# A hybrid encoder block: the rounded weight chunks at places of their own in the line, and the fetch of h's sums on GpSimd's queue

## The chip, the cores and the metric

The kernel runs on one core of a Trainium2 chip. The metric is the device time of one execution in microseconds. Beside the times there is one profiled execution, from which all rows of the profile come. The engines go by their names in the profile: PE is TensorE's matrix multiplier (PEld its weight load), DVE is VectorE, ACT is ScalarE, POOL is GpSimd, SP is SyncE, which only issues DMAs here. A "q" behind a name (SPq) means the engine's sequencer, which waits and issues.

## What is computed

One layer of a streaming encoder, in float32, for 256 tokens of width 2048. Attention heads and a convolution work side by side on one input projection, and a gated feed-forward part follows:

```
xn   = rms_norm(x) @ w_in                          # 2048 x 5120: q, k, v and the two halves ga, gg
att  = diff_attention(rope(q), rope(k), v)         # 4 heads, block-causal
u    = silu(layer_norm(conv31(ga * sigmoid(gg))))  # 1024 channels, 31 causal taps
h    = x + concat(att, u) @ w_out                  # 2048 x 2048
hn   = rms_norm(h)
y    = h + (silu(hn @ w_gate) * (hn @ w_up)) @ w_down   # 2048 x 5632, 2048 x 5632, 5632 x 2048
```

## The kernel before

All weights are read once, as float32. TensorE multiplies in a rounded float32 form, so each weight chunk `w` is split in two: `whi`, the chunk rounded, and `wlo = w - whi`, its residue; the activations are split in the same way (`xhi`/`xlo`, `ahi`/`alo` and so on). A product is made of three matmuls: hi by hi, lo by hi and hi by lo, the activations stationary and 512 columns of the weights streaming.

The work is a list of 337 **chunks** in a fixed order, and `run_chunks` walks through it. For each chunk `t` it emits the loads, roundings and splits of chunks some steps ahead, then the matmuls of `t`. A *plain* chunk has 128 x 1024 weights (two k-tiles of 512 columns):

- `load_chunk` loads it with one DMA from SyncE's queue into a buffer of the tag `raw` (RAW_BUFS of them). Chunks marked `spare_raw`, every third one in many stretches, take one of the two larger `wb` buffers in its place. In `w_gate`, `w_up` and the last twelve chunks of `w_out` none is marked.
- `round_chunk` copies it to `whi` on ScalarE. For some chunks (`by_dma`) ScalarE also writes the negative to `wlo`, and a DMA from GpSimd's queue adds the raw weights to it from memory, which gives the residue.
- `split_chunk` makes the residue `wlo` on VectorE for the others.
- `multiply` or `multiply_two` runs the matmuls; the first two products read `whi`, the last reads `wlo`.

`whi` and `wlo` have four buffers each (HL_BUFS), taken in turn. A raw buffer is free again once its chunk is split. SyncE works through its DMAs in order and stands still wherever the buffer of the next one is not free.

The layer's feed-forward part works in three groups of 4, 4 and 3 blocks of 512 hidden columns (FGROUPS). Block 0 uses plain chunks; the ten others are *fast blocks*, which use a scheme with seven products for half of the contraction: 4 pair chunks (`s`, 1 MB each, always in `wb`) and 8 plain ones each. After a group come the plain chunks of its `w_down` rows: four output blocks of 512 columns (`n` = 0 to 3), eight chunks each, in the last group six. The activations that these need are the last step of a block: `block_done` makes the gated product in the buffers `sum0` to `sum3`, and `transposed` has TensorE transpose them in two halves (L827), ScalarE round each half (`ahi`, L829) and VectorE make its residue (`alo`, L831). So that the engines stay busy these steps are spread over the chunks that follow (TO_TRANSPOSE and `lag`); the last chunk of the output block of a group is the first that needs the second half.

The running sum of h lies in the output in memory: groups 0 and 1 add their parts to it by accumulating DMAs from GpSimd (L1034). In the last group, `fetch_sums` reads it back into buffers of the tags `sum0` to `sum3` (two for each output block), VectorE adds the product to it in `down_done` (L1043), and a DMA writes the finished columns (L1044, on GpSimd's queue but for the last block). The first fetch stands in the order of work at the fifth chunk of the group's first output block, behind the loads that run two chunks ahead; the later ones each stand at the first chunk of their block:

```
            if g == len(FGROUPS) - 1:
                fetch_at[at + (0 if n else FGROUPS[g] * N // P // NK - 2)] = n
```

All tiles of some size have lengths that are multiples of 512 bytes (LINE is 128 floats), so they lie at the same place of a 512-byte line.

Of the kernel before, what the change touches and what calls it, by code (L numbers as in the profile page):

```python
# [12 lines left out]
F32 = mybir.dt.float32  # L13
F32R = mybir.dt.float32r
# [4 lines left out]
P = 128  # L19
# [12 lines left out]
N = 512  # L32

LINE = 128
# [14 lines left out]
NK = 2  # L49
# [5 lines left out]
CONV_BLOCKS = (1, 1, 2, 2, 2)  # L55

AHEAD = 2
RAW_BUFS = 5
AUX = 4

LAG = (3, 2, 6)
HL_BUFS = 4

KTILE_US = 1.30
TAP_US = 0.396
# [35 lines left out]
def tile_block(  # L101
# [6 lines left out]
    act, dve, pool, pe, sp = nc.scalar, nc.vector, nc.gpsimd, nc.tensor, nc.sync  # L108

    const = ctx.enter_context(tc.tile_pool(name="const", bufs=1))  # L110
    small = ctx.enter_context(tc.tile_pool(name="small", bufs=4))

    lhs = ctx.enter_context(tc.tile_pool(name="lhs", bufs=KD // 2))
    wp = ctx.enter_context(tc.tile_pool(name="wp", bufs=4))
# [141 lines left out]
    def spend(us):  # L256
        credit[0] -= us
# [19 lines left out]
    def block(w, cols, ks, xs, done=None, bkey=None, first=True, last=True, spare=False, cuts=()):  # L277

        ks = list(ks)
        cols = [(cols, N)] if isinstance(cols, int) else cols  # L280
        width = sum(n for _, n in cols)
        bkey = bkey if bkey is not None else ("b", len(chunks))
        i = 0
        cuts = list(cuts)
        while i < len(ks):
            part = ks[i : i + (cuts.pop(0) if cuts else NK * N // width)]
            i += len(part)
            chunks.append(dict(w=w, k0=part[0], nk=len(part), cols=cols, width=width, xs=xs, bkey=bkey,
                               first=part[0] == ks[0] and first, last=last and i == len(ks),
                               done=done if i == len(ks) else None, spare=spare, by_dma=False,  # L290
                               load=load_chunk, round=round_chunk,
                               split=split_chunk, multiply=multiply))
# [11 lines left out]
    def load_chunk(c):  # L304
# [4 lines left out]
        else:  # L309
            c["raw"] = view(wp.tile([P, NK * N], F32, tag="raw", name="raw", bufs=RAW_BUFS))  # L310
        ks = c["ks"] if "ks" in c else range(c["k0"], c["k0"] + c["nk"])
        c["src"] = src = weights([(c["w"], k, col, n) for k in ks for col, n in c["cols"]])
        sp.dma_start(out=c["raw"].rearrange("p k n -> p (k n)"), in_=src)

    def round_chunk(c):
        c["hi"] = c["view"](wp.tile([P, NK * N], F32R, tag="whi", name="whi", bufs=HL_BUFS))
        act.copy(c["hi"], c["raw"])  # L317
        if c["by_dma"]:
            c["lo"] = c["view"](wp.tile([P, NK * N], F32R, tag="wlo", name="wlo", bufs=HL_BUFS))
            act.activation(c["lo"], c["raw"], AF.Copy, scale=-1.0)  # L320
            pool.dma_start(out=c["lo"].rearrange("p k n -> p (k n)"), in_=c["src"].bitcast(F32R), accum_op=ALU.add)

    def split_chunk(c):
        if not c["by_dma"]:
            c["lo"] = c["view"](wp.tile([P, NK * N], F32R, tag="wlo", name="wlo", bufs=HL_BUFS))
            dve.tensor_tensor(c["lo"], c["raw"], c["hi"].bitcast(F32), ALU.subtract)  # L326
            spend(LO_US * c["nk"] * c["width"] / N)

# [55 lines left out]
    def run_chunks():  # L384
# [16 lines left out]
        for t in range(n):  # L401
            load_lead, dma_lead, hi_lead, lo_lead = lead(t)
            while split < min(rounded[0], t + 1 + lo_lead):
                chunks[split]["split"](chunks[split])
                split += 1
            while loaded < min(n, t + 1 + load_lead):
                load(loaded)
                loaded += 1
                if load_lead == lo_lead:
                    do_round(1, loaded)  # L410
                    do_round(0, loaded)
                    chunks[split]["split"](chunks[split])
                    split += 1
            do_round(1, t + 1 + dma_lead)
            do_round(0, t + 1 + hi_lead)
            while split < min(n, t + 1 + lo_lead):
                chunks[split]["split"](chunks[split])
                split += 1
            if t in fetch_at:
                fetch_sums(fetch_at[t])  # L420
            chunks[t]["multiply"](chunks[t])
            if chunks[t].get("prompt") and chunks[t]["done"]:
                resume()
# [537 lines left out]
    def fast_block(j, order, after_down):  # L961

        units, sums = [], {}
        left = dict(s=list(range(NS)), g=list(TWOS), u=list(TWOS))
        for unit in order:
            kind = unit.lower()
            what = left[kind].pop(0)
            c = dict(kind=kind, sums=sums, done=None, first={}, last={})
            if kind == "s":
                c.update(k=what, col=j * N, by_dma=False, load=load_pair, round=round_pair, split=split_pair,  # L970
                         multiply=multiply_pair, uses=[q for q, _, _ in PRODUCTS], products=PRODUCTS)
            else:
                c.update(ks=what, w="w_gate" if kind == "g" else "w_up", nk=2, width=N, cols=[(j * N, N)],
                         by_dma=unit.isupper(),
                         load=load_chunk, round=round_chunk, split=split_chunk, multiply=multiply_two,
                         uses=(Q3, QX) if kind == "u" else (Q2, Q4))
            units.append(c)
        assert not any(left.values())
        if after_down:

            units[0]["products"] = PRODUCTS[4:] + PRODUCTS[:4]
        for q in range(8):
            users = [c for c in units if q in c["uses"]]
            users[0]["first"][q] = users[-1]["last"][q] = True
        [c for c in units if c["kind"] == "s"][-1]["done"] = products_done
        units[-1].update(done=lambda sums: block_done(j, sums), prompt=True)
        chunks.extend(units)
# [33 lines left out]
    def fetch_sums(n):  # L1021
        so_far[n] = []
        for m in range(NM):
            t = ffn["pool"].tile([P, N], F32, tag=f"sum{n % 2 * NM + m}", name="so_far")
            sp.dma_start(out=t, in_=out[m * P : (m + 1) * P, n * N : (n + 1) * N])
            so_far[n].append(t)

    def down_done(g, n, ps):
# [99 lines left out]
```

## Time and profile before

| | |
|---|---|
| median of 3 runs | 1083.91 us (1081.84 to 1084.14) |
| the profiled execution | 1078.51 us, span 1076.7 us |
| granted TensorE clock, mean | 0.995 |
| raw loads (L313) | 295 of 512 KB, median 4.9 us to landing |
| pair loads (L898) | 40 of 1024 KB, median 6.2 us to landing |
| residues by DMA (L321) | 48 of 512 KB, median 8.3 us to landing |
| fetches of h's sums (L1025) | 8 of 256 KB, median 4.4 us to landing |

The span runs from the first to the last instruction; the profiled execution's own time is a little longer. Rows of the timeline begin with the start and the length in microseconds, then engine, line, operation, output and inputs by the program's names; brackets hold how long the engine was idle before, and what ended that. Rows of the waits give the total, the number and the longest wait.

### The profile page before, as it was taken

The numbers are of one execution on the slowest core, as the hardware profiler recorded it, in microseconds if no ns is written. First come the engines' busy times: TensorE is split into PE (matmuls) and PEld (weight loads), VectorE is DVE, ScalarE is ACT, GpSimd is POOL, SyncE is SP. The second block draws the span as 40 slices with busy tenths as digits, with TensorE's granted clock in tenths as the row PEclk, the third lists the DMA queues.
The fourth block names the chain that finished last, engine by engine and source line by source line (L and its number), as shares of the span: only waits on it lengthen the run. The fifth ranks groups of instructions, "written<-read, shape, count | busy, mean of one in ns | idle before, by whom it ended". The sixth has DMA issues, their size and how long they took to land. (4 is left out here: it accounts for less than half of the span.)

```text
span 1076.7 us, 13151 instructions
## 1 busy us (share of the span) xinstructions
PE 1051.7 (98%) x4834; PEld 870.9 (81%) x4834; DVE 801.4 (74%) x979; ACT 618.0 (57%) x811; POOL 110.4 (10%) x155
## 2 busy tenths in 40 slices
PE   8999999999999999999999999999999999999798
PEld 7988888877888887788888878878888878888686
DVE  4799988899666689988644688889745477897353
ACT  6544566756756557757343667586544474765231
POOL 0130112200100100101000111010001010100000
PEclk9999999999999999999999999999999999999899
DMA  9555555344457568898476898988847799887471
GB/s 314 205 176 180 200 189 176 137 176 151 143 190 242 175 228 252 284 304 244 153 232 197 267 295 252 293 221 268 259 157 201 239 277 319 223 273 208 145 278 66
DMA packets 62781, 236.57 MB, mean 220 GB/s; under 512 B 7044, under 2 KB 8510, under 8 KB 57596
## 3 DMA queue, kind: packets, MB, share of 16 engines
q1 hardware_dynamic: 52320, 202.66, 52.1%
q0 software_dynamic: 10336, 33.04, 16.6%
q8 instruction: 38, 0.62, 0.2%
q14 instruction: 27, 0.22, 0.1%
q10 hardware_dynamic: 60, 0.03, 0.0%
HBM read 227.30 MB, written 8.39 MB: 219 GB/s over the span
## 5 line engine op out<-in xcount | busy, mean ns | idle before, releaser
L317 ACT CAST whi<-raw 128x1024 fp32r<-128x1024 f32 (+1 forms) x297 | 305.8, 1050 | 183.2 <-PE acc L357 98.1
L326 DVE TENSOR_TENSOR wlo<-raw,whi 128x1024 fp32r<-128x1024 f32 (+1 forms) x249 | 299.7, 1219 | 142.8 <-ACT whi L317 140.9
L357 PE MATMUL acc<-whi,alo 128*128 128x512 f32 x384 | 150.5, 392 | 6.6 <-DVE alo L831 6.6
L356 PE MATMUL acc<-whi,ahi 128*128 128x512 f32 x384 | 150.4, 392 | 0.0
L356 PE MATMUL acc<-whi,xhi 128*128 128x512 f32 (+1 forms) x352 | 131.0, 378 | 3.2 <-ACT xhi L223 2.4
L357 PE MATMUL acc<-whi,xlo 128*128 128x512 f32 (+1 forms) x352 | 129.5, 374 | 0.5 <-DVE xlo L224 0.4
L949 PE MATMUL q<-whi,chi 128*128 128x512 f32 x320 | 124.7, 390 | 0.0
L950 PE MATMUL q<-whi,clo 128*128 128x512 f32 x320 | 124.6, 389 | 0.0
L932 PE MATMUL q<-wh,fhi 128*128 128x512 f32 x280 | 109.7, 392 | 1.7 <-DVE alo L831 1.7
L934 PE MATMUL q<-wl,fhi 128*128 128x512 f32 x280 | 109.0, 389 | 0.0
L933 PE MATMUL q<-wh,flo 128*128 128x512 f32 x280 | 109.0, 389 | 0.0
L512 DVE SCALAR_TENSOR_TENSOR y<-upad,cw,y 128x256 f32<-128x256 f32 x240 | 103.7, 483 | 4.4 <-ACT y L505 3.9
L362 PE MATMUL acc<-wlo,ahi 128*128 128x512 f32 x384 | 103.6, 391 | 0.0
L911 ACT CAST wh<-wt 128x2048 fp32r<-128x2048 f32 x40 | 76.5, 1912 | 38.3 <-DVE wt L909 37.6
L916 DVE TENSOR_TENSOR wl<-wt,wh 128x2048 fp32r<-128x2048 f32 x40 | 91.7, 2291 | 6.6 <-ACT wh L911 5.9
L915 DVE TENSOR_TENSOR wl<-wb,wh 128x1536 fp32r<-128x1536 f32 x40 | 70.1, 1754 | 27.9 <-ACT wh L910 27.9
L357 PEld LDWEIGHTS acc<-whi,alo 128*128 128x128 f32 x384 | 72.6, 189 | 22.1 <-DVE alo L831 6.9
L362 PE MATMUL acc<-wlo,xhi 128*128 128x512 f32 (+1 forms) x352 | 88.3, 376 | 1.4 <-DVE wlo L326 1.4
L955 PE MATMUL q<-wlo,chi 128*128 128x512 f32 x320 | 86.6, 392 | 2.8 <-DMA wlo<-in_wts_dram 2.8
L356 PEld LDWEIGHTS acc<-whi,ahi 128*128 128x128 f32 x384 | 72.5, 189 | 15.3 <-ACT ahi L829 0.2
L362 PEld LDWEIGHTS acc<-wlo,ahi 128*128 128x128 f32 x384 | 71.7, 188 | 14.6
L356 PEld LDWEIGHTS acc<-whi,xhi 128*128 128x128 f32 x352 | 67.2, 191 | 14.9 <-ACT xhi L223 2.8
(197 smaller groups left out, 1487.2 us busy)
## 6 DMA issues: line engine op xcount, KB each, us to landing
raw<-in_wts_dram SPq DMA_DIRECT2D x295, 512.0 KB, 4.9
wb<-in_wts_dram SPq DMA_DIRECT2D x40, 1024.0 KB, 6.2
wlo<-in_wts_dram POOLq DMA_DIRECT2D x48, 512.0 KB, 8.3
out_dram<-part POOLq DMA_DIRECT2D x16, 256.0 KB, 5.1
out_dram<-h POOLq DMA_DIRECT2D x8, 256.0 KB, 5.9
so_far<-out_dram SPq DMA_DIRECT2D x8, 256.0 KB, 4.4
h<-in_x_dram SPq DMA_DIRECT2D x6, 256.0 KB, 7.6
out_dram<-so_far POOLq DMA_DIRECT2D x6, 256.0 KB, 3.0
```

Source lines behind the costliest of these rows:

```text
L317: act.copy(c["hi"], c["raw"])
L326: dve.tensor_tensor(c["lo"], c["raw"], c["hi"].bitcast(F32), ALU.subtract)
L356: pe.matmul(ps[m], xhi[:, ms], hi[:, j, :], start=c["first"] and j == 0, stop=False)
L357: pe.matmul(ps[m], xlo[:, ms], hi[:, j, :], start=False, stop=False)
L362: pe.matmul(ps[m], xhi[:, ms], lo[:, j, :], start=False, stop=c["last"] and j == nk - 1)
L512: dve.scalar_tensor_tensor(y[:, ct, :], src, wk, y[:, ct, :], ALU.mult, ALU.add)
L916: dve.tensor_tensor(c["lo"][:, :4], c["t"], c["hi"][:, :4].bitcast(F32), ALU.subtract)
L932: pe.matmul(ps, fhi[:, f, p, :], c["hi"][:, w], start=bool(first), stop=False)
L933: pe.matmul(ps, flo[:, f, p, :], c["hi"][:, w], start=False, stop=False)
L934: pe.matmul(ps, fhi[:, f, p, :], c["lo"][:, w], start=False, stop=bool(last))
L949: pe.matmul(ps, x1[:, ms], hi[:, i, :], start=i == 0 and bool(c["first"].get(q)), stop=False)
L950: pe.matmul(ps, x2[:, ms], hi[:, i, :], start=False, stop=False)
```

## The change

The four `whi` and the four `wlo` buffers are now separate tags of one buffer each. Each but one is a line (512 bytes) longer and is used from an offset of its own on: 16, 32, 288 and 352 bytes for `whi`, 0, 256, 384 and 448 bytes for `wlo`. They are taken in the same turn as before. An unused tile of 384 bytes in the first pool moves everything behind it, so that the pools of weights start at a line. RAW_BUFS goes from five to four, which gives the room. The fetch of h's sums in the last group (L1025) is issued by GpSimd's queue in place of SyncE's.

```
-RAW_BUFS = 5
+RAW_BUFS = 4
...
+SHIFTS = dict(whi=(4, 8, 72, 88), wlo=(0, 64, 96, 112))
...
     const = ctx.enter_context(tc.tile_pool(name="const", bufs=1))
+    const.tile([P, 3 * LINE // 4], F32, tag="to_line", name="to_line")
...
+    turns = dict(whi=0, wlo=0)
+
+    def shifted(tag):
+        i = turns[tag] % HL_BUFS
+        turns[tag] += 1
+        o = SHIFTS[tag][i]
+        return wp.tile([P, NK * N + (LINE if o else 0)], F32R, tag=f"{tag}{i}", name=tag, bufs=1)[:, o : o + NK * N]
+
     def round_chunk(c):
-        c["hi"] = c["view"](wp.tile([P, NK * N], F32R, tag="whi", name="whi", bufs=HL_BUFS))
+        c["hi"] = c["view"](shifted("whi"))
         act.copy(c["hi"], c["raw"])
         if c["by_dma"]:
-            c["lo"] = c["view"](wp.tile([P, NK * N], F32R, tag="wlo", name="wlo", bufs=HL_BUFS))
+            c["lo"] = c["view"](shifted("wlo"))
...
     def split_chunk(c):
         if not c["by_dma"]:
-            c["lo"] = c["view"](wp.tile([P, NK * N], F32R, tag="wlo", name="wlo", bufs=HL_BUFS))
+            c["lo"] = c["view"](shifted("wlo"))
...
             t = ffn["pool"].tile([P, N], F32, tag=f"sum{n % 2 * NM + m}", name="so_far")
-            sp.dma_start(out=t, in_=out[m * P : (m + 1) * P, n * N : (n + 1) * N])
+            pool.dma_start(out=t, in_=out[m * P : (m + 1) * P, n * N : (n + 1) * N])
```

## The prediction

> **What bounds the kernel now.** I read the page's head first, then TensorE's waits and the longest holes between matmuls, then the chain that ended last around the longest hole, then SyncE's waits.
>
> ```profile
> span 1076.7 us, 13151 instructions
> ...
> PE 1051.7 (98%) x4834; PEld 870.9 (81%) x4834; DVE 801.4 (74%) x979; ACT 618.0 (57%) x811; POOL 110.4 (10%) x155
> ```
>
> TensorE is busy 98% of the span, so time is won or lost in two ways only: in the 25 us where it has nothing to do, or in what one matmul takes. The windows show where a good part of those 25 us lies (columns: stretch, its length, busy us and count of PE, PEld, DVE, ACT, POOL, granted clock, DMA share, GB/s):
>
> ```profile
> 1011.00:1015.00 4.00, 1.60 (x9) 1.03 (x7) 0.00 (x0) 0.59 (x1) 0.00 (x0) 1.00 0.58 183
> 1015.00:1019.00 4.00, 0.00 (x0) 0.00 (x0) 1.64 (x2) 2.09 (x2) 0.00 (x0) 0.56 0.97 327
> 1019.00:1023.00 4.00, 3.76 (x10) 3.03 (x11) 0.19 (x1) 0.44 (x1) 0.00 (x0) 0.59 1.01 410
> ...
> 1027.00:1072.00 45.00, 45.00 (x200) 37.28 (x199) 19.43 (x20) 13.72 (x13) 2.16 (x4) 1.00 0.46 164
> ```
>
> An undisturbed matmul takes 45.00/200 = 0.225 us. From 1012 to 1019 us there is none, and the granted clock falls to 0.56 and stays low (0.59) behind the hole. The timeline has the edges, the chain has the reason:
>
> ```profile
> 1012.20 0.40 PE L356 MATMUL acc<-whi,ahi 128*128 128x512 f32 x1
> ...
> 1019.24 0.80 PE L357 MATMUL acc<-whi,alo 128*128 128x512 f32 x1 [6.64 <-DVE alo L831]
> ...
> 1022.36 1.09 PE L362 MATMUL acc<-wlo,ahi 128*128 128x512 f32 x4
> ```
>
> ```profile
> 1011.00 0.45 PE ps_a L827 x4
> 1011.45 0.23 SPq L1025
> 1011.73 4.47 DMA raw<-in_wts_dram
> 1016.28 1.05 ACT whi L317
> 1017.40 1.11 issue
> 1018.50 0.69 DVE alo L831
> 1019.24 0.80 PE acc L357
> ```
>
> Backwards: the matmul waits for `alo`, the residue of the last hidden block's transposed activations. VectorE makes it, but in its order a chunk's split stands ahead, which waits for ScalarE's rounding, which waits for a raw chunk that SyncE issued only at 1011.73. Why so late, say SyncE's own rows:
>
> ```profile
> 985.30 0.33 SPq L313 DMA_DIRECT2D raw<-in_wts_dram  x1
> 999.41 12.27 SPq L1025 DMA_DIRECT2D so_far<-out_dram  x2
> 1011.73 0.90 SPq L313 DMA_DIRECT2D raw<-in_wts_dram  x2
> ```
>
> ```profile
> SPq L1025 <- DVE sum L1015: 13.5, 1, 13.5
> SPq L1025 <- PE ps_a L827: 11.6, 1, 11.6
> ```
>
> The first two fetches of h's sums (L1025) want the buffers `sum0` and `sum1`, which hold the last block's gated activations until they are transposed (L827). SyncE waits 13.5 + 11.6 us for that, and the raw loads stand behind it.
>
> **The fetch moves to GpSimd.** SyncE loses eight issues and both waits. The raw load that came at 1011.73 (the second chunk of `w_down`'s second block) then waits for its buffer alone. With four buffers that is the one split four plain-buffer loads earlier, here the split that VectorE ran at 990.48:
>
> ```profile
> 990.48 1.22 DVE L326 TENSOR_TENSOR wlo<-raw,whi 128x1024 fp32r<-128x1024 f32 x1
> ...
> 1011.47 0.59 ACT L829 CAST ahi<-ps_a 128x512 fp32r<-128x512 f32 x1 [3.45 <-PE ps_a L827]
> ...
> 1016.28 1.04 ACT L317 CAST whi<-raw 128x1024 fp32r<-128x1024 f32 x1 [4.23 <-DMA raw<-in_wts_dram]
> ```
>
> ```profile
> raw<-in_wts_dram SPq DMA_DIRECT2D x295, 512.0 KB, 4.9
> ...
> out_dram<-part POOLq DMA_DIRECT2D x16, 256.0 KB, 5.1
> ```
>
> So it is issued at 991.7 and lands by about 997. What is late next: ScalarE's rounding follows `ahi`, which ends at 1011.47 + 0.59 = 1012.06. In the trace the road from the start of that rounding to the matmul takes 1019.24 - 1016.28 = 2.96 us (rounding, split, `alo`). The matmul thus starts at 1015.02 in place of 1019.24: the hole shrinks from 7.04 to 2.82 us, a gain of 4.22 us, and does not close. Behind it seven starts from 1019.24 to 1022.36 took 3.12 us where 7 x 0.225 = 1.58 are due: 1.54 us that the low clock costs. Whether 2.8 us of idling still lowers the clock, two rows bracket:
>
> ```profile
> 411.00:414.00 3.00, 1.29 (x6) 0.77 (x5) 2.93 (x5) 1.06 (x1) 0.00 (x0) 1.00 0.84 167
> 414.00:420.00 6.00, 6.00 (x28) 4.96 (x27) 5.90 (x5) 4.13 (x4) 0.87 (x1) 1.00 0.57 193
> ```
>
> After a hole of 1.71 us in a dense stretch the clock stays at 1.00; after 7 us it is 0.59. The residual hole is nearer to the first, so I count the 1.54 us as won, and keep 0 as the other end. Sum: -5.76 us, between -4.22 and, should the hole close, -8.2 (7.04 - 0.23 + 1.54 = 8.35).
>
> On GpSimd the fetch is queued behind nothing: the residue DMAs of the last fast block are long issued. Behind it stand only the writes of finished columns (L1044), which need the fetch anyway. Its price is lateness: issued at about 1011.5, 5.1 us to landing by GpSimd's nearest row, so there at 1016.6 to 1017.6 with the time that GpSimd takes to issue; VectorE wants it (L1043) when the block's last matmul ends, at 1015.02 + 11 x 0.225 = 1017.5. A tie, and VectorE's wait would push splits that are two chunks (24 matmuls, 5.4 us) early. I count nothing.
>
> The Trainium skill's page "DMA: Bandwidth & Descriptors" ("Issuing engines are not separate DMA queues") says that starting transfers on several engines saves only the sequencer's issuing time, which is small. By that rule the move is worth nothing, since SyncE's issue here is not what TensorE waits for; the rows above disagree, because the 25 us are waits ahead of the issue, in a queue served in order.
>
> **Four raw buffers in place of five.** In the plain stretches every third chunk takes one of two `wb` buffers, so these reach six chunks back; four `raw` buffers, used by the other two of three, reach six back as well. In the fast blocks the order has one `wb` in three too, so again both reach six back. The fifth buffer only lets plain loads go out a chunk or two early. Where plain chunks come without `wb` it counts: the stretch of w_gate and w_up into the first fast block.
>
> ```profile
> 382.45 10.31 SPq L313 DMA_DIRECT2D raw<-in_wts_dram  x4
> 392.82 0.43 SPq L898 DMA_DIRECT2D wb<-in_wts_dram  x1
> ...
> 390.06 5.76 DVE L326 TENSOR_TENSOR wlo<-raw,whi 128x1024 fp32r<-128x1024 f32 x5
> ...
> 400.69 1.49 ACT L910 CAST wh<-wb 128x1536 fp32r<-128x1536 f32 x1 [1.33 <-DMA wb<-in_wts_dram]
> ...
> 413.57 0.50 PE L932 MATMUL q<-wh,fhi 128*128 128x512 f32 x1 [1.71 <-DVE alo L831]
> ```
>
> The four plain loads each wait for one split more. The five splits from 390.06 end 1.15 us apart (5.76/5), the third at about 393.5; the last plain load follows that, and the `wb` load goes out at about 394.0 in place of 392.82. ScalarE waited for this `wb`; the same VectorE queue then leads to the hole before 413.57. I put +1.1 us on the path. Ends: 0 (the queue absorbs it) and 4.9 (the first load's own delay, from 382.45 to about 387.3, if it passes undiminished). Elsewhere ScalarE rarely waits for a load (16 of 297 roundings, one of them in the hole above), and what is rounded a few us late was not due yet:
>
> ```profile
> ACT whi L317 <- DMA raw<-in_wts_dram: 46.5, 16, 5.5
> ```
>
> **The places in the line.** All big tiles lie today at the same place of a 512-byte line (their sizes are multiples of 512 bytes); after, each `whi` and `wlo` has one of its own. ScalarE's and VectorE's work on them is off the path. What counts is the matmuls that stream them:
>
> ```profile
> 0.00:1077.00 1077.00, 593.71 (x2432) 449.03 (x2432) 299.65 (x249) 305.83 (x297) 1.00 0.69 220
> ...
> 0.00:1077.00 1077.00, 322.36 (x1216) 222.28 (x1216) 299.65 (x249) 50.84 (x48) 41.72 (x48) 1.00 0.69 220
> ```
>
> (the first row is of `whi` alone, the second of `wlo`): 3,648 matmuls. Nothing before streams a shifted operand. From one side:
>
> ```profile
> L949 PE MATMUL q<-whi,chi x320: 387/389/481, 397.8 to 996.3; 128*128 128x512 f32 x160
> L512 DVE SCALAR_TENSOR_TENSOR y<-upad,cw,y x240: 466/478/686, 39.8 to 275.5; 128x256 f32<-128x256 f32 x120
> ```
>
> The median matmul is 2 ns above the fastest, so the removal of all disturbance could win 2 ns x 2,432 = 4.9 us at the most. From the other, the nearest row is VectorE's: the taps (L512) read the padded channel at thirty different offsets, and the median stands 12 ns over the fastest, 2.6%; 2.6% of 0.225 us on 3,648 matmuls is 21 us. I take 0: the taps' spread holds all offsets and is small, and matmuls beside busy engines are no slower than others.
>
> **Sum.** -5.76 + 1.1 + 0 = -4.66 us. The profiled run, 1078.51 us, would become 1073.9. It lies 5.4 us below the median of the runs shown, 1083.91; I carry the difference over and forecast **1079.3 us**.
>
> **The rivals.** *No gain:* the hole stays, because something else is as late (the fetch on GpSimd holding VectorE, or the runs without a profile lack this hole), and only the +1.1 remains: 1085.0 us. Against it: the chain names SyncE's wait alone. *Slower, the shifted operand:* a matmul whose stream starts inside a line pays for it, on every one of the 3,648. At the taps' 2.6% it is 1079.3 + 21 = 1100 us; it decides from 4.66/3,648 = 1.3 ns per matmul on. For it: no row shows a shifted stream. Against it: the taps. *Much faster, the shifted operand:* a narrow matmul tells what is fixed in one:
>
> ```profile
> 21.11 0.28 PE L356 MATMUL acc<-whi,xhi 128*128 128x256 f32 x1
> 21.23 0.28 PE L357 MATMUL acc<-whi,xlo 128*128 128x256 f32 x1
> ```
>
> 0.12 us for 256 columns against 0.225 for 512 leaves 0.015 us that does not scale. If equal places cause that, 3,648 x 0.015 = 55 us go: about 1025 us. Against it: the time is as constant beside idle engines as beside busy ones, and a collision would vary. The Trainium skill's page "TensorE: Matmul & The Clock Gate" (Part 1, "Wait — 56ns, not 53.3ns?") gives a warm 512-column matmul 215.7 ns, 2.5 of them fixed, and nothing in it depends on an address; this trace's 225 is above that, and the measurement decides.
>
> **How the numbers follow.** Forecast 0.58, no gain 0.15, slower 0.20, much faster 0.07. The forecast's own range, from its terms (gain 4.2 to 8.3, cost 0 to 4.9), is 1075 to 1085; the whole range, which takes in no gain, small prices of a shifted stream (up to 2.9 ns each) and some gain of it, is 1072 to 1090. A measurement of this kernel tells 0.2%, about 2.2 us, from no change. Faster by more: six sevenths of the forecast and the last case, 0.57. Slower by more: the shifted stream, and some of no gain, 0.25. The rest, 0.18.
>
> **What would show it.** Right: no SyncE row of L1025; the raw load of that chunk issued near 992; one hole of 2.5 to 3 us before L357 in the first block of the last `w_down`, waiting for `alo` behind a split, with the clock at 1.00 after it; the hole near 413 longer by about a microsecond; 0.225 us per matmul. Wrong: matmuls of `whi` that take another time than those of `wh`, a hole of the old length, or new holes at L955 or L910 for want of raw chunks.

## The result and the profile after

| kernel | median | range | ratio to before (95%) |
|---|---|---|---|
| before | 1082.88 us | 1078.55 to 1084.14 | |
| changed | 1097.24 us | 1094.69 to 1099.15 | 1.0156 [1.0127, 1.0185] |

The change makes the kernel 14.4 us slower. The forecast was 4.6 us faster. The profiled execution took 1095.96 us, with these heads of the page:

```profile
span 1094.1 us, 13198 instructions
...
PE 1073.8 (98%) x4834; PEld 874.7 (80%) x4834; DVE 801.4 (73%) x979; ACT 618.4 (57%) x811; POOL 113.2 (10%) x163
```

The span grew by 17.4 us (1094.1 - 1076.7). The same 4,834 matmuls keep TensorE busy 22.1 us longer (1073.8 - 1051.7), and its idle time fell by 4.7 us. So the holes did get smaller, as forecast, and something made the matmuls themselves slower. In the changed kernel the code from `RAW_BUFS` on stands a few lines lower: L356, L357 and L362 are now L367, L368 and L373; L932 to L934 are L943 to L945; L949, L950 and L955 are L960, L961 and L966; L831 is L842.

The hole that the fetch made, in the timeline of TensorE (start, us, engine, line, operation, idle time before it and what ended it), and the clock behind it in the windows:

```profile
1034.41 0.41 PE L367 MATMUL acc<-whi,ahi 128*128 128x512 f32 x1
1037.12 0.50 PE L368 MATMUL acc<-whi,alo 128*128 128x512 f32 x1 [2.31 <-DVE alo L842]
```

```profile
1037.00:1040.00 3.00, 2.88 (x12) 2.36 (x13) 0.54 (x2) 0.95 (x1) 0.00 (x0) 1.00 0.53 175
```

From start to start it is 2.71 us where it was 7.04, and the granted clock behind it is 1.00 in this execution where it was 0.59. Now the matmuls: a dense stretch of the last `w_down`, to be laid beside the 200 in 45 us quoted before, and then the whole run's matmuls that stream `whi` and `wlo`:

```profile
1045.00:1090.00 45.00, 45.00 (x195) 36.13 (x193) 18.71 (x19) 13.28 (x13) 4.38 (x8) 1.00 0.47 170
```

```profile
0.00:1100.00 1100.00, 604.69 (x2432) 448.46 (x2432) 299.65 (x249) 304.99 (x297) 0.99 0.69 215
...
0.00:1100.00 1100.00, 327.69 (x1216) 222.73 (x1216) 299.65 (x249) 50.75 (x48) 41.62 (x48) 0.99 0.69 215
```

195 matmuls in place of 200 at full clock is 0.231 us each in place of 0.225. In the two rows of the whole run, `whi` rises from 593.71 to 604.69 us and `wlo` from 322.36 to 327.69: 16.3 us on 3,648 matmuls, 4.5 ns each. VectorE's own time on these tiles has not moved (299.65 us of splits in both), and ScalarE's hardly (304.99 us of roundings for 305.83). From start to start, over all neighbours in the trace, a matmul of 512 columns that streams `whi` or `wlo` took about 227.3 ns before and 232.4 after. That is the figure used below, the "pitch".

### The profile page after: what moved, and what is told of

Read it like the earlier page. It is cut to its first block, busy times and chain, and to the rows that moved or that the text cites. A ratio compares the mean times of both kernels' runs of the same rounds, so it can differ in the third digit from the quotient of the medians.

```text
span 1094.1 us, 13198 instructions
## 1 busy us (share of the span) xinstructions
PE 1073.8 (98%) x4834; PEld 874.7 (80%) x4834; DVE 801.4 (73%) x979; ACT 618.4 (57%) x811; POOL 113.2 (10%) x163
## 4 chain that ended last, share of the span: by engine, by line
PE 84%; issue 5%; DVE 4%; ACT 3%; DMA 2%; POOL 1%; SPq 0%; DVEq 0%; ACTq 0%; POOLq 0%
PE acc L368 15%; PE acc L367 15%; PE acc L373 15%; PE q L966 6%; PE q L961 6%; PE q L960 6%; PE q L943 6%; PE q L944 6%; PE q L945 6%; DMA raw<-in_wts_dram 1%; ACT whi L328 1%; DVE wlo L337 1%; DMA wlo<-in_wts_dram 1%; PE ps_a L838 1%; DVE y L523 1%
## 5 line engine op out<-in xcount | busy, mean ns | idle before, releaser
L368 PE MATMUL acc<-whi,alo 128*128 128x512 f32 x384 | 151.9, 395 | 2.3 <-DVE alo L842 2.3
L367 PE MATMUL acc<-whi,ahi 128*128 128x512 f32 x384 | 151.6, 395 | 0.0
L367 PE MATMUL acc<-whi,xhi 128*128 128x512 f32 (+1 forms) x352 | 132.2, 382 | 3.6 <-ACT xhi L226 2.9
L368 PE MATMUL acc<-whi,xlo 128*128 128x512 f32 (+1 forms) x352 | 131.0, 378 | 0.4 <-DVE xlo L227 0.4
L961 PE MATMUL q<-whi,clo 128*128 128x512 f32 x320 | 126.4, 395 | 0.0
L960 PE MATMUL q<-whi,chi 128*128 128x512 f32 x320 | 126.3, 395 | 0.0
L943 PE MATMUL q<-wh,fhi 128*128 128x512 f32 x280 | 111.7, 399 | 2.1 <-DVE alo L842 2.1
L944 PE MATMUL q<-wh,flo 128*128 128x512 f32 x280 | 111.5, 398 | 0.0
L945 PE MATMUL q<-wl,fhi 128*128 128x512 f32 x280 | 111.1, 397 | 0.0
L373 PE MATMUL acc<-wlo,ahi 128*128 128x512 f32 x384 | 105.5, 396 | 0.0
L966 PE MATMUL q<-wlo,chi 128*128 128x512 f32 x320 | 88.1, 397 | 4.4 <-DMA wlo<-in_wts_dram 2.4
L373 PE MATMUL acc<-wlo,xhi 128*128 128x512 f32 (+1 forms) x352 | 89.7, 380 | 0.3 <-DVE wlo L337 0.3
L368 PEld LDWEIGHTS acc<-whi,alo 128*128 128x128 f32 x384 | 72.1, 188 | 20.1 <-DVE alo L842 2.6
L367 PEld LDWEIGHTS acc<-whi,ahi 128*128 128x128 f32 x384 | 72.1, 188 | 17.0 <-ACT ahi L840 0.2
L373 PEld LDWEIGHTS acc<-wlo,ahi 128*128 128x128 f32 x384 | 71.6, 188 | 16.3
L367 PEld LDWEIGHTS acc<-whi,xhi 128*128 128x128 f32 x352 | 67.3, 191 | 16.4 <-ACT xhi L226 3.3
```

What stands on the lines that cost most here:

```text
L367: pe.matmul(ps[m], xhi[:, ms], hi[:, j, :], start=c["first"] and j == 0, stop=False)
L368: pe.matmul(ps[m], xlo[:, ms], hi[:, j, :], start=False, stop=False)
L373: pe.matmul(ps[m], xhi[:, ms], lo[:, j, :], start=False, stop=c["last"] and j == nk - 1)
L943: pe.matmul(ps, fhi[:, f, p, :], c["hi"][:, w], start=bool(first), stop=False)
L944: pe.matmul(ps, flo[:, f, p, :], c["hi"][:, w], start=False, stop=False)
L945: pe.matmul(ps, fhi[:, f, p, :], c["lo"][:, w], start=False, stop=bool(last))
```

## The experiments

Each ran beside the kernel before on its chip. The median of before was 1080.97 us in the first group (fetch, raw buffers, places, base), 1080.56 us in the second (spacing, the two pads, the early residue) and 1080.40 us in the third.

**1. The fetch alone.** The kernel before with one line changed:

```
-            sp.dma_start(out=t, in_=out[m * P : (m + 1) * P, n * N : (n + 1) * N])
+            pool.dma_start(out=t, in_=out[m * P : (m + 1) * P, n * N : (n + 1) * N])
```

> The kernel before with the fetch alone on GpSimd's queue, five raw buffers and the old places. By the prediction's sum: 4.2 to 8.3 us faster than before, likeliest 5.8 (0.5%): the 7.0 us hole in the first block of the last w_down shrinks to about 2.8 us and the clock stays up behind it. Rival: the hole only moves (VectorE then waits for the fetch), and the time is that of before.

Measured: 1075.92 us, ratio 0.9954 [0.9940, 0.9968], so 5.0 us faster. The timeline and the windows of this kernel:

```profile
1018.71 0.50 PE L357 MATMUL acc<-whi,alo 128*128 128x512 f32 x1 [2.31 <-DVE alo L831]
```

```profile
1019.00:1023.00 4.00, 4.00 (x19) 3.27 (x19) 1.92 (x3) 1.06 (x1) 0.88 (x2) 1.00 0.00 0
```

The hole is 2.71 us from start to start, and the clock behind it full. The step of the fetch was right in mechanism and size. (The span of this one execution, 1074.4 us, is only 2.3 us shorter than before's. It lost time elsewhere: near 412 us a hole of 1.80 us stood where before had 1.71, and the clock fell to 0.50 behind it.)

**2. Four raw buffers alone.**

```
-RAW_BUFS = 5
+RAW_BUFS = 4
```

> The kernel before with four raw buffers alone. By the prediction's sum: 1.1 us slower, between 0 and 4.9; the hole near 413 us grows by about 1 us and no other. Rival (the raw buffers are the cause): most of the 14 us, with new holes for want of raw chunks.

Measured: 1086.77 us, ratio 1.0056 [1.0040, 1.0072], 5.8 us slower by the medians; the pitch stays at 227.3 ns. It costs five times what was forecast, but it isn't what slows the matmuls. Where it goes, in the timeline of TensorE, first two holes of before and then three of this kernel:

```profile
625.19 1.17 PE L955 MATMUL q<-wlo,chi 128*128 128x512 f32 x4 [1.67 <-DMA wlo<-in_wts_dram]
...
881.79 1.17 PE L955 MATMUL q<-wlo,chi 128*128 128x512 f32 x4 [1.14 <-DMA wlo<-in_wts_dram]
```

```profile
413.44 0.50 PE L932 MATMUL q<-wh,fhi 128*128 128x512 f32 x1 [2.55 <-DVE alo L831]
...
627.46 1.17 PE L955 MATMUL q<-wlo,chi 128*128 128x512 f32 x4 [2.71 <-DMA wlo<-in_wts_dram]
...
885.71 1.16 PE L955 MATMUL q<-wlo,chi 128*128 128x512 f32 x4 [2.12 <-ACT whi L317]
```

The first row's hole, before L932, was 1.71 us before and grew by 0.84; the two before L955 grew by 1.04 and 0.98. Together that is 2.9 us. The window behind the first adds to it:

```profile
414.00:420.00 6.00, 6.00 (x21) 4.76 (x20) 5.90 (x6) 4.12 (x5) 0.87 (x1) 0.72 0.62 197
```

Before there were 28 matmuls at a clock of 1.00 in this window; now there are 21 at 0.72. Seven matmuls of 0.225 us are 1.6 us. With the holes that makes 4.5 us, and the two profiled spans differ by 4.6 (1081.3 and 1076.7). That it comes out so near is partly luck: other holes of the two traces differ by up to 1.5 us either way and nearly cancel. SyncE's own rows (first before, then this kernel) show the loads ahead of the second hole:

```profile
609.46 3.69 SPq L313 DMA_DIRECT2D raw<-in_wts_dram  x2
```

```profile
614.04 4.33 SPq L313 DMA_DIRECT2D raw<-in_wts_dram  x2
```

And GpSimd's, the residue DMA that the matmul waits for:

```profile
617.15 0.87 POOL L321 DMA_DIRECT2D wlo<-in_wts_dram  x1 [0.65 <-ACT wlo L320]
```

```profile
618.38 0.87 POOL L321 DMA_DIRECT2D wlo<-in_wts_dram  x1 [0.65 <-ACT wlo L320]
```

The same for the third hole:

```profile
874.28 0.88 POOL L321 DMA_DIRECT2D wlo<-in_wts_dram  x1 [0.54 <-ACT wlo L320]
```

```profile
877.22 0.88 POOL L321 DMA_DIRECT2D wlo<-in_wts_dram  x1 [0.52 <-ACT wlo L320]
```

Ahead of the second hole this kernel runs 1.23 us behind, and so does the residue DMA. The loads go out 4.58 us later, so 3.35 us of it are their own delay. The matmul starts 8.04 us behind the residue DMA's issue in the one (625.19 - 617.15) and 9.08 in the other. At the third hole it is 7.51 (881.79 - 874.28) and 8.49 (885.71 - 877.22), so that hole too grew by what the residue took longer, though the profile puts its end down to a rounding that ended at the same time. The roundings ahead of these residues are no later than the kernel as a whole; the transfers are longer. The later loads run beside them. That fits a collision of the two on the DMA engines; it was not isolated.

**3. Places and four buffers, with the fetch back on SyncE.** The changed kernel with that one line undone:

```
-            pool.dma_start(out=t, in_=out[m * P : (m + 1) * P, n * N : (n + 1) * N])
+            sp.dma_start(out=t, in_=out[m * P : (m + 1) * P, n * N : (n + 1) * N])
```

> The changed kernel with the fetch back on SyncE: new places, the tile ahead of them, and four raw buffers. If the places cost 5 to 6 ns on each of 3,648 matmuls (start to start 232 ns where 227 stood): 20 us slower than before and 5 to 8 us slower than the changed kernel, with the 7 us hole back. If the fetch on GpSimd is what costs: the time of before.

Measured: 1098.38 us, ratio 1.0163 [1.0148, 1.0178]; that is 17.4 us slower than before, against 20 expected. The matmuls have the changed kernel's pitch, so the fetch has nothing to do with that.

**4. Four buffers and the tile that moves everything to a line start, all places equal.** The line-start tile moves every big tile by 384 bytes; relative to each other nothing moves.

```
+    const.tile([P, 3 * LINE // 4], F32, tag="to_line", name="to_line")
```

> Four raw buffers and the unused tile of 384 bytes alone: all big tiles lie at a line's start in place of 128 bytes behind one, all still at the same place among themselves. Theory P (what counts is that streamed and stationary operand lie at different places of a line): nothing beside the raw buffers' price, 227 ns from start to start. Theory B (the base counts: matmuls of wlo's first buffer, unshifted at a line's start, are slow in the changed kernel too): 231 ns or more, 10 to 20 us slower.

Measured: 1084.84 us, ratio 1.0043 [1.0029, 1.0058], and a pitch of 227.3 ns. The theory of the base falls. The four raw buffers cost 4.6 us in this one by its ratio.

**5. The changed kernel with the lengthened buffers, but all at line starts.**

```
-SHIFTS = dict(whi=(4, 8, 72, 88), wlo=(0, 64, 96, 112))
+SHIFTS = dict(whi=(0, 0, 0, 0), wlo=(0, 0, 0, 0))
```

(A second changed line, not shown, keeps the extra 512 bytes of each buffer that had them, though the shift is nought.)

> The changed kernel with every place at the start of a line: each whi and wlo buffer starts at a multiple of 512 bytes, but keeps a line of its own behind it, so that the buffers lie 4,608 bytes apart (wlo's first and second 4,096) where those of the kernel before lie 4,096 apart. Theory P (the place within the line is what costs): matmuls of whi and wlo go back to about 227.3 ns from start to start, and the time is that of the kernel before less 5.0 us (the fetch) plus 5.8 us (four raw buffers): about 1082. Theory S (the spacing of the buffers costs, whatever the place in a line): they stay at about 232 ns, and the time is that of the changed kernel, about 1097.

Measured: 1079.59 us, ratio 0.9989 [0.9970, 1.0007]. The two rows of the whole run, `whi` and then `wlo`:

```profile
0.00:1100.00 1100.00, 592.51 (x2432) 448.40 (x2432) 299.40 (x249) 305.51 (x297) 0.99 0.68 215
...
0.00:1100.00 1100.00, 323.61 (x1216) 223.07 (x1216) 299.40 (x249) 50.69 (x48) 41.62 (x48) 0.99 0.68 215
```

Both are back where they were before (593.71 and 322.36). All that the change has beside the offsets within the line is here, and it comes out within 0.2% of the kernel before: the fetch's 5 us pay for the raw buffers. The offsets alone make the rest of the change.

**6. 128 bytes ahead of `whi` in the kernel before.** Five raw buffers, fetch on SyncE. What is allocated behind the pad moves along, `whi`, `wlo`, `chi` and `clo` among it; `xhi`, `xlo`, `ahi`, `alo`, `hhi`, `hlo` stay. So one kernel holds the treated matmuls and their control.

```
+    pads = []
...
+        if not pads:
+            pads.append(wp.tile([P, 32], F32, tag="pad", name="pad", bufs=1))
         c["hi"] = c["view"](wp.tile([P, NK * N], F32R, tag="whi", name="whi", bufs=HL_BUFS))
```

> The kernel before, with five raw buffers and the fetch on SyncE, and 128 bytes left free ahead of the first whi buffer: whi, wlo and the buffers allocated behind them start 128 bytes later in a line, while the halves of x, of the hidden blocks and of h, allocated earlier, stay. Spacing stays 4,096. Theory P (a streamed buffer at another place of the line than the stationary one costs): the matmuls whose stationary tile is xhi, xlo, ahi, alo, hhi or hlo, about 2,300 of the 3,648, rise from 227.3 to about 232 ns; those with chi, clo, mahi, malo, mchi, mclo, which were moved along, stay: 2,300 x 4.9 ns = 11 us slower, about 1092. If the place of the streamed buffer by itself counts, all 3,648 rise: about 1098. Theory S (spacing): nothing rises, about 1081.

Measured: 1090.69 us, ratio 1.0089 [1.0066, 1.0111], 9.6 us slower by the ratio. The windows over the whole run for the matmuls with `ahi` (treated) and with `chi` (control), first of before and then of this kernel:

```profile
0.00:1100.00 1100.00, 239.33 (x768) 144.21 (x768) 17.04 (x26) 14.69 (x26) 0.99 0.68 215
...
0.00:1100.00 1100.00, 205.12 (x640) 119.38 (x640) 2.44 (x2) 2.11 (x2) 0.99 0.68 215
```

```profile
0.00:1100.00 1100.00, 243.94 (x768) 145.31 (x768) 17.03 (x26) 14.63 (x26) 1.00 0.67 215
...
0.00:1100.00 1100.00, 205.15 (x640) 119.40 (x640) 2.44 (x2) 2.11 (x2) 1.00 0.67 215
```

`ahi` rises by 4.61 us, 6.0 ns for each of its 768 matmuls; `chi` stays within 0.03 us, though it streams the same moved buffers. The pitch is 232.4 ns where the two places differ and about 227.5 where they are equal. So it is not the place of the streamed tile that costs, but its place against that of the stationary tile.

**7. A whole line ahead of `whi`,** with four raw buffers (the same edit with 128 elements for 32):

> Before with four raw buffers and a whole line (512 bytes) left free ahead of the first whi buffer: same place in the line for all, spacing 4,096, but one line of difference to the stationary halves. Theory P: nothing but the four raw buffers, 227.3 ns and about 1086.8. A rule with a longer period than a line (2,048 bytes, say): the 2,300 matmuls with xhi, xlo, ahi, alo, hhi or hlo rise to about 232 ns: about 1098.

Measured: 1084.89 us, ratio 1.0039 [1.0023, 1.0055], pitch 227.3 ns. Nothing but the price of the four buffers. A difference of a whole line counts as none.

**8. 32 bytes ahead of `whi`** (the same edit with 8 elements):

> As with 128 bytes left free ahead of whi, but 32: the 2,400 matmuls with xhi, xlo, ahi, alo, hhi or hlo have 32 bytes of difference in the line, the others none. If any difference costs the same: about 232.4 ns for these and 10 us slower than before (1091). If the price grows with the distance: between 227.3 and 232.4 ns, at a quarter of the price 1083.

Measured: 1091.46 us, ratio 1.0084 [1.0054, 1.0115], and 233 ns with `ahi`, `xhi` or `hhi` as the stationary tile, 227 with `chi`. The rows of `ahi` and `chi`, to be laid beside those of experiment 6:

```profile
0.00:1100.00 1100.00, 244.42 (x768) 144.59 (x768) 17.04 (x26) 14.66 (x26) 0.99 0.67 215
...
0.00:1100.00 1100.00, 205.06 (x640) 119.38 (x640) 2.44 (x2) 2.12 (x2) 0.99 0.67 215
```

A quarter of the distance costs no less: the price isn't graded by it.

**9. The changed kernel with the places of `whi` alone.**

```
-SHIFTS = dict(whi=(4, 8, 72, 88), wlo=(0, 64, 96, 112))
+SHIFTS = dict(whi=(4, 8, 72, 88), wlo=(0, 0, 0, 0))
```

(The extra 512 bytes are kept as in experiment 5.)

> The changed kernel with the places of whi alone (16, 32, 288 and 352 bytes into a line); wlo starts at line starts, as every stationary tile does. If a matmul's time hangs on its own operands' places, the 1,216 matmuls of wlo go back to about 227.3 ns and those of whi stay at about 232.7: 6 us faster than the changed kernel, about 1091. If a slow stretch hangs over the matmuls behind it (wlo's come in runs of 4 to 8 between those of whi), wlo stays at 231 to 233 ns: about 1096 to 1097.

Measured: 1093.00 us, ratio 1.0109 [1.0082, 1.0135]. By the time alone it stands between the two theories; the window row of `wlo` decides:

```profile
0.00:1100.00 1100.00, 327.69 (x1216) 222.76 (x1216) 299.61 (x249) 50.76 (x48) 41.62 (x48) 0.99 0.68 215
```

`wlo` costs 327.69 us, as in the changed kernel, where its own shifts were there too, and not the 323.61 of experiment 5. Its pitch is 231.8 ns with equal places. Sorted by how many matmuls of equal places have gone by since the last unequal one, from none to eight, the mean pitch is 232.7, 231.6, 231.6, 231.2, 231.1, 228.9, 228.0, 227.2 and 226.7 ns. The first four values are of `wlo`, which comes in runs of four between those of `whi`; the others are of the 39 stretches where `wh` and `wl` of a fast block follow. The slow stretch hangs over some six matmuls, and `wlo`'s runs of four never get out of it. This also explains why in the changed kernel `wlo`'s first buffer, the one with shift 0, is as slow as the others (about 233 ns).

A slow stretch of this kind can be seen in the kernel before as well, where all places are equal: there the first ten matmuls behind each of the 64 blocks of narrow ones (the transposes, mostly) had a mean pitch of 230.9 ns, and those that came later 226.8. So there are two rhythms, and behind such a break TensorE is in the slower one for a while. That unequal places break it anew each time would fit all rows here, but no run shows it.

**10. The changed kernel again, beside these.**

> The changed kernel itself, beside the others on one chip. Two theories on the fetch in it: either it is worth there what it was worth alone (5 us), then the changed kernel is 5 us faster than the version with its places and four raw buffers but the fetch on SyncE: 0.5% nearer to the kernel before, a ratio of 1.0115. Or part of that is lost among slower matmuls: a ratio near 1.015.

Measured: 1094.72 us, ratio 1.0125 [1.0100, 1.0149]. Against experiment 3's ratio of 1.0163 [1.0148, 1.0178] the fetch is worth 0.38% or 4.1 us here; with the first result's ratio for the same kernel, 1.0156, it would be 0.8 us. The ratios are of different groups and each is uncertain by 1.6 to 3 us, so the times do not decide between the two theories. The traces show more. First the hole and the window behind it in experiment 3, then in this execution:

```profile
1031.42 0.41 PE L367 MATMUL acc<-whi,ahi 128*128 128x512 f32 x1
1038.40 0.79 PE L368 MATMUL acc<-whi,alo 128*128 128x512 f32 x1 [6.56 <-DVE alo L842]
```

```profile
1038.00:1042.00 4.00, 3.60 (x9) 2.88 (x10) 0.34 (x1) 0.21 (x1) 0.00 (x0) 0.53 1.02 405
```

```profile
1030.14 0.40 PE L367 MATMUL acc<-whi,ahi 128*128 128x512 f32 x1
1032.86 0.50 PE L368 MATMUL acc<-whi,alo 128*128 128x512 f32 x1 [2.31 <-DVE alo L842]
```

```profile
1033.00:1037.00 4.00, 4.00 (x11) 3.14 (x12) 0.43 (x1) 1.05 (x1) 0.00 (x0) 0.57 0.39 131
```

The hole is 6.98 us without the fetch's move and 2.72 with it, so 4.26 us are won among the slower matmuls too. But here the clock fell to 0.57 behind the short hole, where it stayed at 1.00 in the first execution of the same kernel. The part of the gain that the clock makes is a matter of the execution.

**11. The fetch, and the residue ahead of the split.** Experiments 1 and 2 point to a better kernel: old places, five raw buffers, fetch on GpSimd. The hole of 2.71 us that is left is `alo` behind a split in VectorE's order. Beside the line of experiment 1, in the generator of the transposes the last block's `alo` is made one step earlier:

```
-            yield from lag(2)
+            yield from lag(1 if j == sum(FGROUPS) - 1 else 2)
```

> Before with the fetch on GpSimd and, for the last hidden block alone, alo made one step earlier in VectorE's order, so that it no longer stands behind a chunk's split. The hole of 2.71 us that the moved fetch leaves ahead of L357 near 1016 us should shrink to about 0.5 us: about 2 us faster than the fetch alone, near 1074 (0.6% faster than before). Rival: the split that now comes later is wanted just as early, and its own matmuls (L362) wait 2 us instead: no gain over the fetch alone, 1076.

Measured: 1073.26 us, ratio 0.9927 [0.9908, 0.9947]: 7.3 us faster than before, the fastest of all.

```profile
1015.07 0.39 PE L356 MATMUL acc<-whi,ahi 128*128 128x512 f32 x1
1015.96 0.50 PE L357 MATMUL acc<-whi,alo 128*128 128x512 f32 x1 [0.50 <-DVE alo L831]
```

TensorE waits 0.50 us for `alo` where it waited 2.31, and the split that comes later is not missed.

## Why the prediction was wrong

**The fetch was right.** Forecast -5.76 us (between -4.22 and -8.2) and a hole of 2.82 us; measured -5.0 us alone and a hole of 2.71, in the changed kernel as well. (By the prediction's own sum the outer end is -8.35; -8.2 is a slip.) The 1.54 us for the lowered clock were in part luck: behind the hole of 2.31 us of idling the clock stayed full in four traces and fell in a fifth (experiment 10). The fetch's own lateness cost nothing, as assumed: VectorE's add into `so_far` waits for TensorE's sums, not for the transfer:

```profile
1039.52 1.28 DVE L1054 TENSOR_TENSOR so_far<-so_far,acc 128x512 f32<-128x512 f32 x2 [2.46 <-PE acc L373]
```

The Trainium skill's rule in "DMA: Bandwidth & Descriptors" ("Issuing engines are not separate DMA queues") gave nought for this step; the 5.0 us measured speak for the rows, that is for the waits in a queue served in order.

**The four raw buffers were mis-sized.** The term was +1.1 us, with ends at 0 and 4.9. Three kernels put it at 6.1, 4.6 and 4.2 us by their ratios, near the upper end or beyond it. The path that the prediction named gave about what it said: the hole near 413 grew by 0.84 us. Two things were missing. The prediction looked only at late roundings ("what is rounded a few us late was not due yet"); at 625 and 882 us the holes before L955 wait for a residue DMA, and each landed about 1 us later behind its issue. And a longer hole can bring the lowered clock with it, 1.6 us behind the first one, which the prediction had counted for the fetch and not here.

**The places were the step that failed.** The term was taken as 0, with an upper end of +21 us. It measured 5.1 ns of pitch, which on 3,648 matmuls is 18.6 us if the narrow ones are counted like the others; the times give 1.0125 or 1.0156 with the offsets against 0.9989 without, 14.7 to 18 us. The sign that the prediction had named for being wrong is there: matmuls of `whi` take another time than those of `wh` (pitch about 232.7 and 228.1 ns). The rival "slower, the shifted operand" (1100 us, given 0.20) is what came. Its price of 5.8 ns was close by luck, since it came from the spread of VectorE's taps. Its mechanism was only half right: the kernels with pads show that a shifted stream costs nothing by itself if the stationary tile is shifted with it.

Two arguments had set the likelier end at 0. The taps' spread says how VectorE fares with its operands at offsets; it bears on no other engine. And that matmuls beside busy engines are no slower than beside idle ones excludes a collision with other engines. It says nothing of TensorE's own two reads, the streamed tile and the next stationary one, which go on side by side through the run (PE is busy for 98% of the span, PEld for 81%). In the trace of before all those tiles had equal places, so it could not show the price, and a median 2 ns above the fastest was a sign of an undisturbed rhythm rather than of an insensitive one. That read the length of single matmuls; their distance from start to start had the two rhythms of experiment 9 in it, 4 ns apart. Its bounds, -4.9 and +21, lay 26 us apart where all else came to 4.66, and 0 was no measured value of it; the forecast's own range of 1075 to 1085 left it out.

The rival "much faster" falls with the same rows: equal places are the fast case. The 0.225 us of a dense stretch are not caused by them. The Trainium skill's page "TensorE: Matmul & The Clock Gate" (Part 1, "Wait — 56ns, not 53.3ns?") gives 215.7 ns and no dependence on an address; here it is 227.3 ns with equal places and 232.4 with unequal ones.

## What to carry to other kernels

Where TensorE is the bound, keep the tiles that it streams and the tiles that it loads as stationary at the same place of a 512-byte line: sizes in multiples of a line do it, and a small tile allocated in between undoes it (here 0.8% for 32 bytes). Whether half a line is enough was not isolated: a difference of 256 bytes stood only among other unequal ones. A DMA that must wait belongs on a queue where nothing that is due stands behind it. When the trace holds a resource in one state only, its silence is no evidence of a price near nought: bound the price, and when the bound outweighs the rest of the sum, let the chances say so.

## What the runs showed of the hardware that was not expected

A matmul of 128x512 in this kernel takes 227.3 ns from start to start when the streamed and the stationary tiles have equal places within 512 bytes, and about 232.4 ns otherwise. 32 and 128 bytes cost about the same, a whole line costs nothing, and the effect hangs over some six matmuls. The Trainium skill's page "SBUF — State Buffer" ("SBUF: two separate sides") says that TensorE's accesses never wait on anyone; the control in experiment 6 shows that they can depend on how TensorE's own operands lie. Why, the runs do not tell: that the two reads meet in the memory is an inference.

The clock behind a hole does not follow from the hole's length alone. The changed kernel had the same hole of 2.31 us in both of its traces, with the clock at 1.00 behind it in one and at 0.57 in the other. In experiment 11 TensorE was idle for 1.85 us near 412 and the clock fell; in experiment 5 it was idle for 2.33 us at the same place and it stayed full. The hole and the window behind it, first of experiment 11, then of experiment 5:

```profile
412.24 0.50 PE L932 MATMUL q<-wh,fhi 128*128 128x512 f32 x1 [1.85 <-DVE alo L831]
```

```profile
414.00:420.00 6.00, 6.00 (x23) 4.82 (x23) 5.90 (x5) 4.12 (x4) 0.87 (x1) 0.82 0.81 255
```

```profile
415.42 0.50 PE L943 MATMUL q<-wh,fhi 128*128 128x512 f32 x1 [2.33 <-DVE alo L842]
```

```profile
416.00:422.00 6.00, 6.00 (x28) 4.98 (x27) 5.90 (x6) 4.01 (x5) 0.87 (x1) 1.00 0.58 196
```

The Trainium skill's page "TensorE: Matmul & The Clock Gate" (Part 1, "What's actually happening") lowers the clock after an idle window of about 3.4 us, and says that this window runs freely. That the moment of a hole decides as well as its length agrees with a window that runs freely; that 1.85 us of idling are enough does not agree with 3.4 us, and here the measurement decides. Over all thirteen traces, their first 100 us left out, the clock fell behind 16 of the 30 holes between 1.8 and 2.8 us. The prediction's reading, that a hole nearer to 1.7 us than to 7 keeps the clock, held for its own hole in four traces of five and is no rule.
